# Moving six of eight single-token state steps of a Mamba-2 mixer from its own stage into six heads of the other mixer

## The chip, the cores and the metric

One Trainium2 chip, one core of it. The metric is the time of one execution on the device in microseconds. Of the kernel before there are three runs: median 1763.9 us, 1761.53 to 1765.04.

## What is computed

One decoder layer, fp32, for a prompt of 1024 tokens and for 8 sampled tokens (one new token each of 8 requests with states of their own): norm, one input projection into 6656 columns and 16 dt columns, two mixers side by side (HGRN2 with 8 heads, Mamba-2 with 16 heads of 64 in 2 groups), their gated norms, an output projection, a gated MLP with a causal convolution, a final norm. What matters here is the Mamba-2 step of the sampled tokens and the gate behind it. In the names of the kernel, for each pair of state-space heads j (0 to 7, four per group g):

```
state[b]  = state[b] * exp(dt*A)[b] + (dt*x)[b] outer B[g, b]      # 128 rows (2 heads x 64) by 128, b = 0..7
y[b]      = state[b] . C[g, b] + D * x[b]
gated     = y * silu(z)                                            # prompt columns likewise
mix       = gated * rsqrt(mean over the group's 512 rows of gated^2 + eps) * norm_w
```

The new states are an output (ssm_sample), and mix goes into the output projection with the HGRN2 heads' rows.

## The kernel before

Activations lie with channels on partitions and tokens along the free dimension: 1024 prompt columns and behind them 8 columns of the sampled tokens, 1032 in all, in three chunks of 344. Each weight tile comes as fp32, is split into a rounded part and a rest (L190 on ACT, L192 on DVE), and a product is three matmuls (L93). So an input job, 128 output columns, is 72 matmuls of 344 columns.

TensorE (PE) has an order written out by hand: a list of jobs, with streams of other work driven between their matmuls at a fixed number of pieces per matmul. The jobs are x8 and x10, x0 to x3, x9, x11, x4 to x7 (columns of x, B and C, with a convolution and a Silu at each job's end), z0 to z3, then f, q, v, sg of HGRN2 head 0, z4 to z7, then f to sg of heads 1 to 7, then the output projection (o8, o12, o0, o4), up, down and the last norm. `ssd(0)`, the chunked state-space scan of group 0, is driven beside x9 to x7; `ssd(1)` beside z0 to v0. `head(h)` is driven beside the input jobs of head h+1; head 7 beside the first output jobs. DVE, ACT and POOL get their order from the scheduler. Loads by `fetch` stand on the SP queue behind the last weight load.

In a chunk of the scan (`ssd_front`, `ssd_back`): xp is a transposed x tile, xdt its product with dt (L557), bt B and C products, csb the decay matrix (loaded, L541 and L546 on ACT, L560 on DVE), yo the part of the carried state, ecs its scaling (L577, L593), st the new state part, S the carried state (L583), yd the part within the chunk.

`ssm_decode(g, i)` (L628 to L647) is the step of the sampled tokens for j = 4g + i. In two halves of four tokens each it loads a state Sd and broadcast rows Bb and Cb (256 KB each), scales Sd on ACT (L641, four instructions), multiplies Bb (L642) and adds it to Sd (L643) on DVE, writes Sd, multiplies Cb on POOL (L645) and reduces it on DVE (L646); L647 adds D*x. It is called at the begin of x5, x7, z0 and z1 for group 0, and at that of z4 to z7 for group 1. `ssm_gate(g)` multiplies with silu(z) in the z jobs (L675, L676), all 1032 columns, and norms them.

A head with its decode rows goes: sample states of HGRN2 (Sh, L864 to L868), gates by halving (tt, L885 to L891), attention blocks a and am (L910 to L949), decode outputs od and odr (L956), kt and kv (L963 to L977) into the states SS, odp (L984), o from am, vt, q and SS, and the norm (hr_d, L999 to L1023). Tiles of the tag "e" (two, 1060 wide) carry wide rows in the x stage and in the first head; those of the tag "d" (four) carry a head's sample rows.

Of the kernel before, what the change touches and what calls it, by code (L numbers as in the profile page):

```python
# [39 lines left out]
QW = NT // 4  # L40
# [10 lines left out]
def hybrid_layer(  # L51
# [9 lines left out]
    V, A, G, PE, SP = nc.vector, nc.scalar, nc.gpsimd, nc.tensor, nc.sync  # L61
# [5 lines left out]
    dram = ctx.enter_context(tc.tile_pool(name="dscr", bufs=1, space=DRAM))  # L67
# [21 lines left out]
    def bank(s, tag="mx"):  # L89
        return psmx.tile([P, 512], F32, tag=tag, bufs=NBANK[tag], name=nm(s))  # L90

    def mm(out, lhsT, rhs, start=True, stop=True):
        PE.matmul(out, lhsT, rhs, start=start, stop=stop)  # L93
# [55 lines left out]
    def col(name, i=0):  # L149
        c = vlay[name] + i  # L150
        return vcol[:, c:c + 1]
# [20 lines left out]
    def fetch(dst, src):  # L172

        with tc.issue_after(last_w[0].ins):
            SP.dma_start(dst, src)
# [179 lines left out]
    def xbc_evict(j, ext, c, cs, ps):  # L355
        e = min(cs.stop, T)
        A.copy(ext[:, 3 + cs.start:3 + e], ps[:, :e - cs.start])
        if c == 2:
            V.tensor_copy(ext[:, 3 + T:3 + T + 32].rearrange("p (b r) -> p b r", r=4)[:, :, 3:4],
                          ps[:, T - cs.start:].unsqueeze(2))  # L360
            V.tensor_copy(last11[:, j, :], ps[:, CH - 11:])

    def xbc_close(j, ext):
        G.tensor_copy(ext[:, 3 + T:3 + T + 32].rearrange("p (b r) -> p b r", r=4)[:, :, 0:3],
                      bufT[:, j, :].rearrange("p (b r) -> p b r", r=3))
        n = T + 32
        acc = tl("big", "xbc")
        conv_tail(acc, ext, 4, "cw", "cb", j, XT, n)
        A.activation(acc[:, :T], acc[:, :T], AF.Silu)
        A.activation(acc[:, T:NT], acc[:, T + 3:T + 32:4], AF.Silu)  # L370
        return acc

    def xbc_job(j, put):
        ext = []
        def begin():
            ext.append(xbc_open())
            if j in (5, 7):
                ssm_decode(0, (5, 7).index(j))

        in_job(f"x{j}", OFF_X + j * P, lambda c, cs, ps: xbc_evict(j, ext[0], c, cs, ps), begin=begin, end=lambda: put(xbc_close(j, ext[0])))  # L380

# [20 lines left out]
    ones = keep.tile([P, P], F32, name="ones")  # L402
# [24 lines left out]
    for c, cs in enumerate(chunks):  # L427
        ps = psmm.tile([P, 512], F32, tag="mm", name=nm("dt"))
# [7 lines left out]
    dps = bank("dps", "nx")  # L436
# [177 lines left out]
    def d4(t):  # L614
        return t.rearrange("p (b n) -> p b n", n=P)
# [12 lines left out]
    def ssm_decode(g, i):  # L628
        j = g * 4 + i
        xdd = small.tile([P, 2, ND], F32, tag="xdd", name=nm("xdd"))  # L630
        xdec = Xg[g][i][:, T:NT]
        V.tensor_tensor(xdd[:, 0, :], xdec, ddb[:, 0, j, :], op=ALU.mult)
        for b0 in (0, 4):
            bs = slice(b0, b0 + 4)
            Bb, Cb = tl("d", "Bb")[:, :512], tl("d", "Cb")[:, :512]
            for t_, r in ((Bb, 2 * g), (Cb, 2 * g + 1)):
                fetch(t_, bc_d[r, bs].rearrange("b n -> (b n)").unsqueeze(0).to_broadcast([P, 512]))
            Sd = tl("ld", "Sd")
            fetch(d4(Sd), state_ssm[0, bs, 2 * j:2 * j + 2].rearrange("b h p n -> (h p) b n"))
            for b in range(4):  # L640
                A.activation(d4(Sd)[:, b, :], d4(Sd)[:, b, :], AF.Copy, scale=ddb[:, 1, j, b0 + b:b0 + b + 1])  # L641
            V.tensor_tensor(d4(Bb), d4(Bb), cb(xdd[:, 0, bs]), op=ALU.mult)  # L642
            V.tensor_tensor(Sd, Sd, Bb, op=ALU.add)  # L643
            SP.dma_start(ssm_sample[0, bs, 2 * j:2 * j + 2].rearrange("b h p n -> (h p) b n"), d4(Sd))
            G.tensor_tensor(Cb, Sd, Cb, op=ALU.mult)  # L645
            V.tensor_reduce(xdd[:, 1, bs], d4(Cb), axis=mybir.AxisListType.X, op=ALU.add)  # L646
        V.scalar_tensor_tensor(xdec, xdec, d_bc[:, j:j + 1], xdd[:, 1, :], op0=ALU.mult, op1=ALU.add)  # L647

    def rstd_of(dst, tmp, ps, n):

        A.activation(dst, ps, AF.Abs_reciprocal_sqrt, bias=epsc, scale=1.0 / n)
        V.scalar_tensor_tensor(tmp, ps, n * EPS, dst, op0=ALU.add, op1=ALU.mult)
        V.scalar_tensor_tensor(tmp, tmp, -0.5 / n, dst, op0=ALU.mult, op1=ALU.mult)
        V.scalar_tensor_tensor(dst, tmp, 1.5, dst, op0=ALU.add, op1=ALU.mult)

    gr_d = dram.tile([2, 4, QW], F32, name="gr_d")

    def ssm_gate(g):
        acc = []

        def z_job(i):
            j = g * 4 + i

            def begin():
                if i == 0:
                    acc.append(tl("g", "gacc"))
                if g:
                    ssm_decode(1, i)
                elif i < 2:
                    ssm_decode(0, i + 2)  # L670

            def evict(c, cs, ps):
                Y = Xg[g][i][:, cs]
                sz = tl("z", "sz")[:, :CH]
                A.activation(sz, ps, AF.Silu)  # L675
                V.tensor_tensor(Y, Y, sz, op=ALU.mult)  # L676
                if i == 0:
                    A.activation(acc[0][:, cs], Y, AF.Square)
                else:
                    A.activation(sz, Y, AF.Square)  # L680
                    (V if g or i == 3 else G).tensor_tensor(acc[0][:, cs], acc[0][:, cs], sz, op=ALU.add)
                if i == 3 and c == NCH - 1:
                    after(36, rstd)
            in_job(f"z{j}", OFF_Z + j * P, evict, begin=begin)

        def rstd():
            ps = bank("ms", "nx")
            for q in range(4):
                mm(ps[32 * q:32 * q + 32, :QW], ones[:, 0:32], acc[0][:, q * QW:(q + 1) * QW])
            nt = tl("z", "nt")  # L690
            rstd_of(nt[:, :QW], tl("z", "nt")[:, :QW], ps[:, :QW], 512)
            SP.dma_start(gr_d[g], nt[::32, :QW])
            after(36, rows)

        def rows():
            fetch(acc[0][:, :NT], gr_d[g].rearrange("a t -> (a t)").unsqueeze(0).to_broadcast([P, NT]))
            after(20, lambda: spread(tail(), 6))

        def tail():
            for i in range(4):  # L700
                j = g * 4 + i
                Y = Xg[g][i][:, :NT]
                V.scalar_tensor_tensor(Y, Y, col("sn", j), acc[0][:, :NT], op0=ALU.mult, op1=ALU.mult)
                SP.dma_start(mix_d[8 + j], Y)
                yield

        for i in range(4):
            z_job(i)
# [132 lines left out]

    def head(h, t):
        f, k, q, v, sg = (t[n] for n in ("f", "k", "q", "v", "sg"))


        dps = bank("vd", "nx")
        PE.transpose(dps[:ND, :P], v[:, T:NT], ident)
# [11 lines left out]
        for b0 in (0, 4):  # L859
            bs = slice(b0, b0 + 4)  # L860
            ds = slice(T + b0, T + b0 + 4)
            Sd, vb = tl("ld", "Sh"), tl("d", "vb")[:, :512]
            fetch(d4(Sd), state_hgrn[0, bs, h].rearrange("b k v -> k b v"))
            fetch(vb, vd_d[h, bs].rearrange("b n -> (b n)").unsqueeze(0).to_broadcast([P, 512]))  # L864
            G.tensor_tensor(d4(vb), d4(vb), cb(k[:, ds]), op=ALU.mult)
            V.tensor_tensor(d4(Sd), d4(Sd), cb(f[:, ds]), op=ALU.mult)
            G.tensor_tensor(Sd, Sd, vb, op=ALU.add)
            SP.dma_start(hgrn_sample[0, bs, h].rearrange("b k v -> k b v"), d4(Sd))  # L868
            Sds.append(d4(Sd))

# [75 lines left out]
        scale(6, pair[1], pair[1])  # L946
        for b in (0, 64):
            A.copy(am[b:b + 32, :, b + 32:b + 64], c32(ps[:, :256])[b:b + 32])
        A.copy(am[0:64, :, 64:P], p6[0:64, :].rearrange("p (c t) -> p c t", t=64))  # L949
# [6 lines left out]
        V.tensor_copy(odr, ops[:, :P])  # L956
        yield 3.5

        for hf in range(2):
# [24 lines left out]
        V.tensor_copy(od[:, 0, :], dps[:, :ND])  # L984
        A.activation(od[:, 1, :], dps[:, :ND], AF.Square)
        yield 3.2


        for hf in range(2):
# [529 lines left out]
```

## Time and profile before

| | |
|---|---|
| median of 3 runs | 1763.9 us |
| the profiled execution | 1764.9 us, of it 1763.2 us of span |
| PE busy | 1709.8 us (97%) |
| DVE, ACT, POOL busy | 1097.8, 778.7, 478.8 us |
| mean granted clock of TensorE | 0.995 |
| waits of PE between 160 and 240 us | 8.0 us in five |
| waits of PE between 440 and 800 us | 0.8 us in one |
| longest wait of PE between 800 and 1000 us | 4.5 us |

A row of the waits reads: engine, line, what it waited for, total us, times, longest us. A row of a timeline reads: start in us, duration in us, engine, line, operation, out<-in, shape, count, and in brackets the idle time of the engine ahead of it with what ended it. A row of the windows has the stretch, its length, then busy us and instructions (x) of PE, PEld (weight loads), DVE, ACT and POOL, then the granted clock of TensorE, the share of the DMA engines and GB/s. SPq is the queue of SP that issues DMAs.

### The profile page before, as it was taken

What the parts mean: (1) busy time and instruction counts of PE and PEld (TensorE: products, weight loads), DVE (VectorE), ACT (ScalarE), POOL (GpSimd) and SP (SyncE); (2) the same over time, 40 slices, a digit from 0 to 9 for tenths busy, and PEclk for the clock granted to TensorE, in tenths of its full rate; (3) what the DMA queues carried; (4) which work ended last, traced back from release to release, by engine and by line L of the source; (5) the groups of instructions that cost most, each with busy time, mean ns of one, the idle gap of its engine ahead of it and who ended that gap; (6) DMA issues with size and microseconds to landing.
All of it is one profiled execution on the core that took longest, in us unless ns stands there. A gap on an engine that the chain in (4) does not pass through costs nothing. (4 is left out here: it accounts for less than half of the span.)

```text
span 1763.2 us, 38543 instructions
## 1 busy us (share of the span) xinstructions
PE 1709.8 (97%) x16115; PEld 1659.4 (94%) x16115; DVE 1097.8 (62%) x1978; ACT 778.7 (44%) x1422; POOL 478.8 (27%) x485
## 2 busy tenths in 40 slices
PE   7999899999999999999799999999999999999998
PEld 6998789899999999999799989999999999999997
DVE  6668966566554554566636687776667767445545
ACT  7577686444434344344423374343333434111114
POOL 2103231111110110111220355666666664000002
PEclk9999999999999999999999999999999999999999
DMA  5355644553232332234336832222222226422312
GB/s 166 65 148 149 173 120 143 167 169 120 83 93 57 98 87 72 77 110 144 114 115 210 250 123 73 73 85 82 88 73 73 79 82 214 153 83 78 98 61 97
DMA packets 250132, 200.23 MB, mean 114 GB/s; under 512 B 47252, under 2 KB 220870, under 8 KB 249942
## 3 DMA queue, kind: packets, MB, share of 16 engines
q1 hardware_dynamic: 249670, 197.68, 37.0%
q8 instruction: 126, 2.06, 0.5%
q14 instruction: 48, 0.39, 0.1%
q0 software_dynamic: 288, 0.10, 0.0%
HBM read 155.17 MB, written 46.95 MB: 115 GB/s over the span
## 5 line engine op out<-in xcount | busy, mean ns | idle before, releaser
L93 PE MATMUL mm<-hl,wh 128*128 128x344 f32 x1248 | 406.1, 326 | 0.0
L93 PE MATMUL mm<-hh,wh 128*128 128x344 f32 x1248 | 405.6, 326 | 0.0
L93 PE MATMUL mm<-hh,wl 128*128 128x344 f32 x1248 | 402.8, 323 | 0.8 <-issue 0.8
L93 PEld LDWEIGHTS mm<-hl,wh 128*128 128x128 f32 x1248 | 236.1, 189 | 4.8 <-issue 4.2
L93 PEld LDWEIGHTS mm<-hh,wh 128*128 128x128 f32 x1248 | 236.1, 189 | 4.2 <-issue 3.4
L93 PEld LDWEIGHTS mm<-hh,wl 128*128 128x128 f32 x1248 | 236.3, 189 | 1.4 <-issue 1.2
L190 ACT CAST wh<-ws 128x1024 fp32r<-128x1024 f32 x96 | 100.6, 1048 | 254.9 <-PE dn L93 134.9
L93 PE MATMUL ub<-uh,wh 128*128 128x258 f32 x704 | 199.5, 283 | 4.2 <-DVE fext L1332 2.7
L93 PE MATMUL ub<-uh,wl 128*128 128x258 f32 x704 | 198.7, 282 | 0.0
L93 PE MATMUL ub<-ul,wh 128*128 128x258 f32 x704 | 198.6, 282 | 0.0
L93 PE MATMUL dn<-ah,wh 128*128 128x256 f32 (+1 forms) x640 | 181.1, 283 | 2.0 <-DVE x L1449 2.0
L93 PE MATMUL dn<-al,wh 128*128 128x256 f32 (+1 forms) x640 | 180.6, 282 | 0.0
L93 PE MATMUL dn<-ah,wl 128*128 128x256 f32 (+1 forms) x640 | 180.1, 281 | 0.0
L192 DVE TENSOR_TENSOR wl<-ws,wh 128x1024 fp32r<-128x1024 f32 x88 | 108.8, 1236 | 78.5 <-ACT wh L190 77.7
L93 PE MATMUL ua<-uh,wh 128*128 128x258 f32 x528 | 149.3, 283 | 1.5 <-DVE val L1344 1.3
L93 PE MATMUL mm<-mh,wh 128*128 128x258 f32 x512 | 146.9, 287 | 3.0 <-ACT x L1077 1.8
L93 PE MATMUL ua<-ul,wh 128*128 128x258 f32 x528 | 149.1, 282 | 0.0
L93 PE MATMUL ua<-uh,wl 128*128 128x258 f32 x528 | 148.4, 281 | 0.0
L93 PE MATMUL mm<-ml,wh 128*128 128x258 f32 x512 | 145.4, 284 | 0.9 <-DVE ml L1037 0.9
L93 PE MATMUL mm<-mh,wl 128*128 128x258 f32 x512 | 145.2, 284 | 0.0
L93 PEld LDWEIGHTS ub<-uh,wh 128*128 128x128 f32 x704 | 133.0, 189 | 4.9 <-DVE fext L1332 2.9
L1282 DVE TENSOR_TENSOR wl<-wt,wh 128x512 fp32r<-128x512 f32 x88 | 89.1, 1031 | 73.8 <-ACT wh L1281 73.8
(353 smaller groups left out, 3981.9 us busy)
## 6 DMA issues: line engine op xcount, KB each, us to landing
ws<-in_w_in_dram SPq DMA_DIRECT2D x52, 512.0 KB
ws<-in_w_up_dram SPq DMA_DIRECT2D x44, 512.0 KB
ws<-in_w_out_dram SPq DMA_DIRECT2D x24, 512.0 KB
act_d<-val SPq DMA_DIRECT2D x22, 516.0 KB
al<-act_d SPq DMA_DIRECT2D x22, 516.0 KB
ws<-in_w_down_dram SPq DMA_DIRECT2D x22, 512.0 KB
ml<-mix_d SPq DMA_DIRECT2D x48, 172.0 KB
csb<-cs_d SPq DMA_DIRECT2D x32, 256.0 KB
```

The source lines that it names most:

```text
L93: PE.matmul(out, lhsT, rhs, start=start, stop=stop)
L190: A.copy(wh[:, :n], ws[:, :n])
L192: V.tensor_tensor(wl[:, :n], ws[:, :n], wh[:, :n].bitcast(F32), op=ALU.subtract)
L1282: V.tensor_tensor(lo[:, cs], sums[name], hi[:, cs].bitcast(F32), op=ALU.subtract)
```

## The change

The sampled tokens' columns leave the wide tiles: the Silu of the convolution writes them into a small tile xdk, silu(z) of those columns goes into szd by a POOL copy in the last chunk of each z job, and the wide gate covers 1024 columns. Two decodes (j = 0 and 1) remain `ssm_decode`, at the begin of z4 and z6. The other six run as `decode_beside` in heads 1 to 6: in one width of 1024 (Sd and Bb in the two "e" tiles, Cb in two "d" tiles); the loads behind the head's last write of HGRN2 sample states, the multiplies and the add behind odr and am, the reduces behind the od copy. After the fourth of a group (heads 2 and 6) `decode_gate` gates its columns, and 80 pieces later `decode_norm` norms them (matmul dgs) and writes them into mix_d. The diff, cut to its core:

```diff
+    xdk = const.tile([P, 8, ND], F32, name="xdk")
+    szd = const.tile([P, 8, ND], F32, name="szd")
...
-        A.activation(acc[:, T:NT], acc[:, T + 3:T + 32:4], AF.Silu)
+        A.activation(xdk[:, j, :] if j < 8 else acc[:, T:NT], acc[:, T + 3:T + 32:4], AF.Silu)
...
-            if j in (5, 7):
-                ssm_decode(0, (5, 7).index(j))
...
+    def decode_beside(g, i):
+
+        j = g * 4 + i
+        xdd = small.tile([P, 2, ND], F32, tag="xdd", name=nm("xdd"))
+        xdec = xdk[:, j, :]
+        Sd, Bb = tl("e", "Sd")[:, :T], tl("e", "Bb")[:, :T]
+        Cb = [tl("d", "Cb")[:, :512] for _ in range(2)]
...
+        def load(behind):
+            with tc.issue_after(behind.ins):
+                SP.dma_start(d8(Sd), state_ssm[0, :, 2 * j:2 * j + 2].rearrange("b h p n -> (h p) b n"))
+                SP.dma_start(Bb, bc_d[2 * g].rearrange("b n -> (b n)").unsqueeze(0).to_broadcast([P, T]))
+                for q in range(2):
+                    SP.dma_start(Cb[q], bc_d[2 * g + 1, 4 * q:4 * q + 4].rearrange("b n -> (b n)").unsqueeze(0).to_broadcast([P, 512]))
...
+        def front(behind, behind_a):
+            V.tensor_tensor(xdd[:, 0, :], xdec, ddb[:, 0, j, :], op=ALU.mult)
+            with tc.issue_after(behind.ins):
+                V.tensor_tensor(d8(Bb), d8(Bb), xdd[:, 0, :].unsqueeze(2).to_broadcast([P, ND, P]), op=ALU.mult)
+            for b in range(ND):
+                with tc.issue_after(behind_a.ins):
+                    A.activation(d8(Sd)[:, b, :], d8(Sd)[:, b, :], AF.Copy, scale=ddb[:, 1, j, b:b + 1])
+            V.tensor_tensor(Sd, Sd, Bb, op=ALU.add)
+            SP.dma_start(ssm_sample[0, :, 2 * j:2 * j + 2].rearrange("b h p n -> (h p) b n"), d8(Sd))
+            for q in range(2):
+                G.tensor_tensor(Cb[q], Sd[:, q * 512:(q + 1) * 512], Cb[q], op=ALU.mult)
...
+        def back(behind):
+            for q in range(2):
+                with tc.issue_after(behind.ins):
+                    V.tensor_reduce(xdd[:, 1, 4 * q:4 * q + 4], d4(Cb[q]), axis=mybir.AxisListType.X, op=ALU.add)
+            V.scalar_tensor_tensor(xdec, xdec, d_bc[:, j:j + 1], xdd[:, 1, :], op0=ALU.mult, op1=ALU.add)
+            if i == 3:
+                decode_gate(g)
...
+    def decode_gate(g):
+        js = slice(4 * g, 4 * g + 4)
+        dg = small.tile([P, 6, ND], F32, tag="dg", bufs=1, name=nm("dg"))
+        V.tensor_tensor(xdk[:, js, :], xdk[:, js, :], szd[:, js, :], op=ALU.mult)
+        V.tensor_tensor(dg[:, 0:4, :], xdk[:, js, :], xdk[:, js, :], op=ALU.mult)
+        V.tensor_reduce(dg[:, 4, :], dg[:, 0:4, :].rearrange("p j b -> p b j"), axis=mybir.AxisListType.X, op=ALU.add)
+        after(80, lambda: decode_norm(g, js, dg))
+
+    def decode_norm(g, js, dg):
+        ps = bank("dgs", "nx")
+        mm(ps[:, :ND], ones, dg[:, 4, :])
+        rstd_of(dg[:, 4, :], dg[:, 5, :], ps[:, :ND], 512)
+        for j in range(js.start, js.stop):
+            V.scalar_tensor_tensor(xdk[:, j, :], xdk[:, j, :], col("sn", j), dg[:, 4, :], op0=ALU.mult, op1=ALU.mult)
+        SP.dma_start(mix_d[8 + js.start:8 + js.stop, :, T:NT].rearrange("j p b -> p j b"), xdk[:, js, :])
...
-                if g:
-                    ssm_decode(1, i)
-                elif i < 2:
-                    ssm_decode(0, i + 2)
+                if g and i % 2 == 0:
+                    ssm_decode(0, i // 2)
...
+                if c == NCH - 1:
+                    G.tensor_copy(szd[:, j, :], sz[:, n:])
...
+        step_ = decode_beside((h + 1) // 4, (h + 1) % 4) if 1 <= h <= 6 else None
...
+            step_[0](kept_)
...
+            step_[1](held, turned_)
...
+            step_[2](held)
```

PE's order differs only in two added matmuls dgs and in widths of the gate's norm. What moves on the others, first on DVE beside the scan of group 0 (jobs x6 and x7): xbc are x tiles, S and ecs as above. Before:

```order
L596 SCALAR_TENSOR_TENSOR xbc_1184<-xbc_1184,d_bc,ecs_1921 128x128
L643 TENSOR_TENSOR Sd_2098<-Sd_2098,Bb_2094 128x512
L643 TENSOR_TENSOR Sd_2113<-Sd_2113,Bb_2109 128x512
L646 TENSOR_REDUCE xdd_2092<-Cb_2095 128x4
L646 TENSOR_REDUCE xdd_2092<-Cb_2110 128x4
L647 SCALAR_TENSOR_TENSOR xbc_992<-xbc_992,d_bc,xdd_2092 128x8
L632 TENSOR_TENSOR xdd_2478<-xbc_1184,ddb 128x8
L583 TENSOR_TENSOR S_2042<-S_2042,st_2040 128x512
L577 TENSOR_TENSOR ecs_2031<-yo_2034,ecs_2031 128x512
L552 TENSOR_TENSOR bt_1991<-bg_1988,tri 128x128
```

and now, the same chunk:

```order
L597 SCALAR_TENSOR_TENSOR xbc_1186<-xbc_1186,d_bc,ecs_1890 128x128
L553 TENSOR_TENSOR bt_1960<-bg_1957,tri 128x128
L561 TENSOR_TENSOR csb_1943<-csb_1943,bt_1960 128x512
L561 TENSOR_TENSOR csb_1949<-csb_1949,bt_1960 128x512
L584 TENSOR_TENSOR S_2011<-S_2011,st_2009 128x512
L578 TENSOR_TENSOR ecs_2000<-yo_2003,ecs_2000 128x512
L594 TENSOR_TENSOR ecs_2000<-yd_2014,ecs_2000 128x512
```

Adds, reduces and the small steps of the decode are gone between the xbc steps and S, and bt and csb now stand ahead of S.

Second, ACT in head 2, from the last am copy to the norm of the head. Before:

```order
L949 COPY am<-a_749_6122 64x8x64
L831 ACTIVATE v_6170<-mm_6171 128x344
L964 COPY kt_6205<-ktp_6206 128x512
L964 COPY kt_6212<-ktp_6213 128x512
L831 ACTIVATE v_6170<-mm_6197 128x344
L985 ACTIVATE od_6270<-odp_6268 128x8
L190 CAST wh_6298<-ws_6297 128x1024
```

and now:

```order
L1010 COPY am<-a_717_5969 64x8x64
L674 ACTIVATE Sd_5490<-Sd_5490,ddb 128x128 x8
L890 ACTIVATE v_6031<-mm_6032 128x344
L1027 COPY kt_6066<-ktp_6067 128x512
L1027 COPY kt_6073<-ktp_6074 128x512
L890 ACTIVATE v_6031<-mm_6058 128x344
L1048 ACTIVATE od_6131<-odp_6129 128x8
L190 CAST wh_6159<-ws_6158 128x1024
```

The eight scales of the state stand between am and the eviction of v, ahead of both kt copies.

Third, DVE in head 2 in the SS steps behind kv. Before:

```order
L977 SCALAR_TENSOR_TENSOR SS_6247<-SS_6247,tt_5688,kv_6248 128x128 x2
L984 COPY od_6270<-odp_6268 128x8
L977 SCALAR_TENSOR_TENSOR SS_6247<-SS_6247,tt_5688,kv_6248 128x128
L1013 SCALAR_TENSOR_TENSOR sg_5520<-od_6270,vcol,sg_5520 128x8
L977 SCALAR_TENSOR_TENSOR SS_6257<-SS_6247,tt_5688,kv_6258 128x128
L977 SCALAR_TENSOR_TENSOR SS_6257<-SS_6257,tt_5688,kv_6258 128x128 x3
```

and now:

```order
L1040 SCALAR_TENSOR_TENSOR SS_6108<-SS_6108,tt_5535,kv_6109 128x128 x2
L1047 COPY od_6131<-odp_6129 128x8
L1040 SCALAR_TENSOR_TENSOR SS_6108<-SS_6108,tt_5535,kv_6109 128x128
L683 TENSOR_REDUCE xdd_5489<-Cb_5492 128x4
L1040 SCALAR_TENSOR_TENSOR SS_6118<-SS_6108,tt_5535,kv_6119 128x128
L683 TENSOR_REDUCE xdd_5489<-Cb_5493 128x4
L1040 SCALAR_TENSOR_TENSOR SS_6118<-SS_6118,tt_5535,kv_6119 128x128
L684 SCALAR_TENSOR_TENSOR xdk<-xdk,d_bc,xdd_5489 128x8
L1040 SCALAR_TENSOR_TENSOR SS_6118<-SS_6118,tt_5535,kv_6119 128x128
L693 TENSOR_TENSOR xdk<-xdk,szd 128x32
L1078 SCALAR_TENSOR_TENSOR sg_5355<-od_6131,vcol,sg_5355 128x8
L1040 SCALAR_TENSOR_TENSOR SS_6118<-SS_6118,tt_5535,kv_6119 128x128
```

The two reduces, the step of D and the first step of the gate now stand among the SS steps. (The wide multiply and the wide add stand further ahead, on both sides of the step qb that follows odr.)

More of the change, by code (lines that the diff above doesn't have):

```diff
@@ L630, in ssm_decode @@
         xdd = small.tile([P, 2, ND], F32, tag="xdd", name=nm("xdd"))
-        xdec = Xg[g][i][:, T:NT]
+        xdec = xdk[:, j, :]
         V.tensor_tensor(xdd[:, 0, :], xdec, ddb[:, 0, j, :], op=ALU.mult)
@@ L647, in ssm_decode, with d8 @@
         V.scalar_tensor_tensor(xdec, xdec, d_bc[:, j:j + 1], xdd[:, 1, :], op0=ALU.mult, op1=ALU.add)
+    def decode_beside(g, i):
+        j = g * 4 + i
+        xdd = small.tile([P, 2, ND], F32, tag="xdd", name=nm("xdd"))
+        xdec = xdk[:, j, :]
+        Sd, Bb = tl("e", "Sd")[:, :T], tl("e", "Bb")[:, :T]
+        Cb = [tl("d", "Cb")[:, :512] for _ in range(2)]
+        def d8(t):
+            return t.rearrange("p (b n) -> p b n", n=P)
+        def load(behind):
[22 more added lines that the diff above has]
+                decode_gate(g)
+        return load, front, back
@@ L654, in rstd_of @@
         V.scalar_tensor_tensor(dst, tmp, 1.5, dst, op0=ALU.add, op1=ALU.mult)
-    gr_d = dram.tile([2, 4, QW], F32, name="gr_d")
+    gr_d = dram.tile([2, 4, 256], F32, name="gr_d")
     def ssm_gate(g):
@@ L666, in begin @@
                     acc.append(tl("g", "gacc"))
-                if g:
-                    ssm_decode(1, i)
-                elif i < 2:
-                    ssm_decode(0, i + 2)
+                if g and i % 2 == 0:
+                    ssm_decode(0, i // 2)
             def evict(c, cs, ps):
+                cs = slice(cs.start, min(cs.stop, T))
+                n = cs.stop - cs.start
                 Y = Xg[g][i][:, cs]
@@ L675, in evict @@
                 A.activation(sz, ps, AF.Silu)
+                if c == NCH - 1:
+                    G.tensor_copy(szd[:, j, :], sz[:, n:])
+                sz = sz[:, :n]
                 V.tensor_tensor(Y, Y, sz, op=ALU.mult)
@@ L688, in rstd @@
             for q in range(4):
-                mm(ps[32 * q:32 * q + 32, :QW], ones[:, 0:32], acc[0][:, q * QW:(q + 1) * QW])
+                mm(ps[32 * q:32 * q + 32, :256], ones[:, 0:32], acc[0][:, q * 256:(q + 1) * 256])
             nt = tl("z", "nt")
-            rstd_of(nt[:, :QW], tl("z", "nt")[:, :QW], ps[:, :QW], 512)
-            SP.dma_start(gr_d[g], nt[::32, :QW])
+            rstd_of(nt[:, :256], tl("z", "nt")[:, :256], ps[:, :256], 512)
+            SP.dma_start(gr_d[g], nt[::32, :256])
             after(36, rows)
         def rows():
-            fetch(acc[0][:, :NT], gr_d[g].rearrange("a t -> (a t)").unsqueeze(0).to_broadcast([P, NT]))
+            fetch(acc[0][:, :T], gr_d[g].rearrange("a t -> (a t)").unsqueeze(0).to_broadcast([P, T]))
             after(20, lambda: spread(tail(), 6))
@@ L701, in tail @@
                 j = g * 4 + i
-                Y = Xg[g][i][:, :NT]
-                V.scalar_tensor_tensor(Y, Y, col("sn", j), acc[0][:, :NT], op0=ALU.mult, op1=ALU.mult)
-                SP.dma_start(mix_d[8 + j], Y)
+                Y = Xg[g][i][:, :T]
+                V.scalar_tensor_tensor(Y, Y, col("sn", j), acc[0][:, :T], op0=ALU.mult, op1=ALU.mult)
+                SP.dma_start(mix_d[8 + j][:, :T], Y)
                 yield
@@ L867, in head @@
             G.tensor_tensor(Sd, Sd, vb, op=ALU.add)
-            SP.dma_start(hgrn_sample[0, bs, h].rearrange("b k v -> k b v"), d4(Sd))
+            kept_ = SP.dma_start(hgrn_sample[0, bs, h].rearrange("b k v -> k b v"), d4(Sd))
             Sds.append(d4(Sd))
+        if step_:
+            step_[0](kept_)
         hb = [slice(0, 512), slice(512, T)]
@@ L948, in head @@
             A.copy(am[b:b + 32, :, b + 32:b + 64], c32(ps[:, :256])[b:b + 32])
-        A.copy(am[0:64, :, 64:P], p6[0:64, :].rearrange("p (c t) -> p c t", t=64))
+        turned_ = A.copy(am[0:64, :, 64:P], p6[0:64, :].rearrange("p (c t) -> p c t", t=64))
         ops = bank("od", "nx")
@@ L955, in head @@
         odr = small.tile([P, P], F32, tag="odr", bufs=1, name=nm("odr"))
-        V.tensor_copy(odr, ops[:, :P])
+        held = V.tensor_copy(odr, ops[:, :P])
+        if step_:
+            step_[1](held, turned_)
         yield 3.5
@@ L983, in head @@
         od = small.tile([P, 3, ND], F32, tag="dsq", name=nm("od"))
-        V.tensor_copy(od[:, 0, :], dps[:, :ND])
+        held = V.tensor_copy(od[:, 0, :], dps[:, :ND])
         A.activation(od[:, 1, :], dps[:, :ND], AF.Square)
         yield 3.2
+        if step_:
+            step_[2](held)
         for hf in range(2):
```

## Prediction

> **What bounds the kernel now.** I read the page first, then the waits of PE in stretches of the program, then the windows for the clock, then the timelines of DVE and ACT around each wait.
>
> ```profile
> span 1763.2 us, 38543 instructions
> PE 1709.8 (97%) x16115; PEld 1659.4 (94%) x16115; DVE 1097.8 (62%) x1978; ACT 778.7 (44%) x1422; POOL 478.8 (27%) x485
> ```
>
> PE is busy for all but 53.4 of 1763.2 us, and the change leaves its matmuls nearly as they are. So the only time to be won is where PE waits, and where its clock is cut. The waits of PE from 160 to 240 us (the state-space chunks beside x9 to z0), then the longest of 800 to 1000 us (it is in head 7):
>
> ```profile
> PE yo L93 <- DVE S L583: 2.0, 1, 2.0
> PE xp L555 <- ACT xbc L369: 2.0, 1, 2.0
> PE yd L93 <- DVE xdt L557: 1.5, 1, 1.5
> PE bg L548 <- DVE S L583: 1.3, 1, 1.3
> PE xp L555 <- DVE ecs L577: 1.2, 1, 1.2
> ...
> PE xtd L810 <- DVE odr L956: 4.5, 1, 4.5
> ```
>
> The five waits before 240 us sum to 8.0 us. What the waits do to the clock stands in the windows (the column behind POOL is the granted clock):
>
> ```profile
> 172.00:176.00 4.00, 2.85 (x27) 2.68 (x28) 3.96 (x5) 2.01 (x5) 2.49 (x2) 1.00 0.52 107
> 205.00:209.00 4.00, 2.43 (x10) 1.35 (x10) 4.00 (x7) 1.15 (x3) 1.88 (x2) 0.81 0.12 18
> 209.00:213.00 4.00, 4.00 (x29) 3.42 (x29) 3.79 (x8) 0.11 (x1) 1.77 (x2) 0.76 0.40 114
> 226.00:229.00 3.00, 1.36 (x6) 1.36 (x7) 0.93 (x2) 2.97 (x5) 0.00 (x0) 0.83 0.87 175
> 229.00:232.00 3.00, 3.00 (x13) 3.00 (x13) 0.18 (x1) 2.96 (x5) 1.04 (x1) 0.60 0.55 164
> 440.00:800.00 360.00, 359.16 (x4837) 345.06 (x4836) 183.72 (x350) 154.44 (x254) 31.43 (x24) 1.00 0.29 85
> ```
>
> Around the wait of 1.5 us (yd, at 173) the clock stays at 1.00. After each wait of 2.0 us it is cut: 4 × 0.19 + 4 × 0.24 = 1.7 us are lost at 205 to 213, and 3 × 0.17 + 3 × 0.40 = 1.7 us at 226 to 232. The five waits cost 8.0 + 3.4 = **11.4 us** together. In heads 1 to 6, the last row, PE is without work for 0.8 of 360 us, DVE works 184, ACT 154, POOL 31, and DMA has a share of 0.29.
>
> [...]
>
> **What each wait hangs on.** DVE, then ACT, at those places:
>
> ```profile
> 171.80 0.69 DVE L642 TENSOR_TENSOR Bb<-Bb,xdd 128x512 f32<-128x512 f32 x1 [2.83 <-DMA Bb<-bc_d]
> 172.41 0.68 DVE L557 TENSOR_TENSOR xdt<-xp,dt 128x512 f32<-128x512 f32 x1
> ...
> 185.56 1.28 DVE L643 TENSOR_TENSOR Sd<-Sd,Bb 128x512 f32<-128x512 f32 x2
> 188.03 0.69 DVE L646 TENSOR_REDUCE xdd<-Cb 128x4 f32<-128x512 f32 x1 [1.19 <-POOL Cb L645]
> 190.28 0.69 DVE L646 TENSOR_REDUCE xdd<-Cb 128x4 f32<-128x512 f32 x1 [1.56 <-POOL Cb L645]
> ...
> 191.34 0.68 DVE L583 TENSOR_TENSOR S<-S,st 128x512 f32<-128x512 f32 x1
> ...
> 193.34 1.28 DVE L560 TENSOR_TENSOR csb<-csb,bt 128x512 f32<-128x512 f32 x2
> ...
> 198.68 2.10 DVE L347 SCALAR_TENSOR_TENSOR xbc<-ext,vcol,xbc 128x1056 f32<-128x1056 f32 x1
> ...
> 203.32 1.30 DVE L347 SCALAR_TENSOR_TENSOR xbc<-ext,vcol,xbc 128x1056 f32<-128x1056 f32 x1
> ...
> 205.75 0.67 DVE L583 TENSOR_TENSOR S<-S,st 128x512 f32<-128x512 f32 x1
> ```
> ```profile
> 218.14 0.99 ACT L641 ACTIVATE Sd<-Sd,ddb 128x128 f32<-128x128 f32 x3 [0.94 <-DMA Sd<-in_state_ssm_dram]
> ...
> 220.55 0.39 ACT L641 ACTIVATE Sd<-Sd,ddb 128x128 f32<-128x128 f32 x1
> 221.61 1.28 ACT L541 ACTIVATE csb<-csb,cst 128x128 f32<-128x128 f32 x4 [0.68 <-DMA csb<-cs_d]
> ...
> 226.53 1.06 ACT L369 ACTIVATE xbc<-xbc 128x1024 f32<-128x1024 f32 x1
> ```
>
> - yd, 1.5 us: xdt stands behind a decode multiply that waited 2.83 us for its transfer. Without it xdt can start up to 2.8 us earlier, and the wait goes whole: 1.5.
> - xp behind ecs, 1.2 us: DVE again, 6 us on, with a conv step ahead of ecs that stays. I count 1.0 of it (0 to 1.2).
> - bg, 1.3 us: S at 191.34 stands behind the Sd adds (1.28), two reduces (1.38) and their waits for POOL (1.19 + 1.56), some 5.4 us of decode. In the new order bt and csb stand ahead of that S, 1.28 us and a small step, which leaves 3.8 us for a wait of 1.3. It goes whole: 1.3.
> - yo, 2.0 us: S at 205.75 stands behind the backlog of that, two more Bb multiplies (0.69 each), and conv steps stretched from 1.30 to 2.10. The conv steps stay. I count 1.7 of it (1.0 to 2.0); a rest of 0.3 costs no clock, so its 1.7 us of clock go too.
> - xp behind the Silu of x7, 2.0 us: four decode scales (0.99 + 0.39) and a wait of 0.94 go from ACT, 2.3 us, but the csb scales also wait for a transfer and may not come all of that earlier. I count 1.3 (0 to 2.0). The rest of 0.7 is below the waits that left the clock at 1.00, so 1.7 us of clock go.
>
> Sum: 1.5 + 1.0 + 1.3 + 1.7 + 1.3 = 6.8, with the clock 6.8 + 3.4 = **10.2 us** (if each counts at its low end, and one clock cut stays, 3.8 + 1.7 = 5.5; at the high end 11.4). Decodes also leave z5 and z7; no wait of PE hangs on them, so nothing. The two decodes left, beside z4 and z6, stand where two stood before. The small copies of eight gate columns on POOL, and the gate's passes over 1024 instead of 1032 columns, lie beside z jobs that show no wait for POOL: nothing.
>
> **What the heads have to take.** Each of heads 1 to 6 gets one decode. DVE, ACT, then PE and the DMA queue in head 2, which stands for the six:
>
> ```profile
> 549.36 0.69 DVE L866 TENSOR_TENSOR Sh<-Sh,f 128x512 f32<-128x512 f32 x1 [1.68 <-DMA Sh<-in_state_hgrn_dram]
> ...
> 557.53 0.17 DVE L984 COPY od<-odp 128x8 f32<-128x8 f32 x1
> ...
> 558.01 1.49 DVE L977 SCALAR_TENSOR_TENSOR SS<-SS,tt,kv 128x128 f32<-128x128 f32 x4
> ```
> ```profile
> 545.89 0.58 ACT L949 COPY am<-a 64x512 f32<-64x512 f32 x1
> 550.25 0.46 ACT L831 ACTIVATE v<-mm 128x344 f32<-128x344 f32 x1 [3.78 <-PE mm L93]
> 551.79 1.08 ACT L964 COPY kt<-ktp 128x512 f32<-128x512 f32 x2 [1.09 <-PE ktp L963]
> ```
> ```profile
> 555.42 1.95 PE L93 MATMUL kv<-vt,kt 128*128 128x128 f32 x16
> ...
> 562.47 0.39 PE L93 MATMUL o<-q,SS 128*128 128x128 f32 x2
> ```
> ```profile
> 525.10 3.22 SPq L868 DMA_DIRECT2D out_dram<-Sh  x2
> ...
> 546.08 1.86 SPq L175 DMA_DIRECT2D Sh<-in_state_hgrn_dram  x2
> ```
>
> ACT: eight scales of 0.39, 3.1 us, in a gap of 3.78 us behind am. They end at 549.6, before the eviction of v at 550.25 and kt behind it. DVE: the multiply and the add of twice the width (about 2 × 0.64 = 1.3 us each) fall beside gaps; the add ends near 550.9. POOL is idle and multiplies until 553.6. The reduces come behind the od copy at 557.5: two at 0.69 and a small step or three put 1.4 to 2.0 us among the SS steps, which end at 559.5 now and near 561.5 then. The first matmul that needs SS starts at 562.47, so the margin is 1 us and the work is **hidden: 0**. If that cover were gone, each us beyond it would stand in the way of PE.
>
> The loads are issued behind the Sh write, at 528.3, and wanted at 546.5: 18 us for 1.5 MB. Two Sh loads (0.5 MB) issued from 546.08 held DVE until 549.36 and 550.80, so 0.5 MB take at most 4.7 us and three times that 14.1 us. They land by 542.5. The w_in load behind them on SP's queue still has its time, since the DMA share is 0.29.
>
> The gate of four decodes adds, after heads 2 and 6, one matmul 128x8 (0.22 us a piece by the odp group, at most twice that with its weights), a table load and some eight DVE steps of 0.2 us.
>
> ```profile
> L93 PE MATMUL odp<-selod,odr x10: 175/216/256, 493.9 to 740.1; 128*128 128x8 f32 x10
> ```
>
> I count 0.4 us for the two matmuls. In head 3 the rest lies on engines that are idle half of the time, so nothing. In head 7 the small steps fall among the chain to odr (the 4.5 us wait), where DVE has hardly a gap:
>
> ```profile
> 834.00 2.56 DVE L1037 TENSOR_TENSOR ml<-ml,mh 128x344 fp32r<-128x344 f32 x3 [1.41 <-ACT mh L1036]
> ```
>
> They cost some 1.6 us ahead of a gap of 1.41 us, which takes them up, and one transpose of xs now stands ahead of that chain instead of in it. I take **0**, between −2 us (the transpose and a little of the wait saved) and +2 us (the steps added whole to the chain).
>
> Sum: 10.2 − 0.4 = **9.8 us** saved. The profiled execution took 1764.9 us (1763.2 of span and 1.7 around it), 1.0 above the median; so 1755.1 on its scale and **1754** on that of the median, 1763.9.
>
> **Rivals.**
> - *The waits stay in part.* Conv steps, evictions and csb multiplies still share DVE before 240 us, and POOL still stretches conv steps from 1.30 to 2.10. With each wait at its low end (5.5, less 0.4) it is 1759.
> - *The clock does not come back.* If it is cut there for something other than the two waits (PE has sparse stretches on either side of them), only the waits go: 1754 + 3.4 = 1757.5. Against it stands that it is 1.00 around yd's wait at 173, in the same kind of stretch. [...]
> - *Slower: a late state holds ACT in the heads.* The eight scales stand ahead of v and kt on ACT. If the state lands at 552.7 instead of 542.5, the scales end at 555.8, v and the kt copies (0.46 + 1.08) at 557.4, and kv, which starts at 555.42 now, waits 2.0 us. With the clock cut behind it that is 3.7 us a head, 22 us for six: **1776**. It decides from a landing at 550.7, 22 us after the issue; the Sh loads took 3 to 5 us, which speaks against it, and four loads in a row on one queue, with w_in behind them, speak for it.
> - *It is given back.* The change removes the waits, but head 7 gets longer (its DVE is full from 834 to 857, and the write of xdk stands between ml loads on SP's queue), by 5 us or more, or the freed DVE meets the next late transfer: 1762, no change.
>
> **Chances.** Forecast 0.54 (own range 1750.5 to 1757.5), partial 0.14, clock not back 0.05, given back 0.10, slower 0.17 (a third of it a milder case, one or two heads, near 1768). A measurement of this kernel can tell about 0.2%, 3.5 us, from no change. Faster by more than that takes the forecast, the clock case and nearly all of the partial case, 0.12 of it: 0.71. Same: the rest of that and the given back, 0.12. Slower: 0.17. The range goes from 1750 (all 11.4 and 2 in head 7 would be 1750.9) to 1765, which takes in the partial case and the one where all is given back and leaves out the slower ones.
>
> **What would show it.** Right: in 160 to 240 us the waits on L557 and S are gone, PE's clock is 0.97 or more, and head 2's PE waits for no engine. Wrong: a wait of o or kv on SS or kt in the heads, with DVE's reduces idle before them on Cb; a Sd scale waiting for its transfer ahead of v; xtd's wait in head 7 above 6.5 us; or the same waits before 240 us held by conv steps.

## The result, and the profile after

| | before | after |
|---|---|---|
| the runs known at the prediction, median | 1763.9 us (3 runs) | |
| all runs beside the result, median | 1766.75 us (8 runs) | 1754.27 us (8 runs) |
| ratio, with its 95% interval | | 0.9935, 0.9917 to 0.9953 |
| span of the profiled execution | 1763.2 us | 1752.2 us |

The forecast was 1754. From the profile page of the changed kernel:

```profile
span 1752.2 us, 38536 instructions
PE 1707.5 (97%) x16119; PEld 1659.1 (95%) x16119; DVE 1099.7 (63%) x1986; ACT 782.7 (45%) x1427; POOL 484.3 (28%) x493
```

PE's busy time fell by 2.3 us, the span by 11.0: the rest is idle time of PE that is gone. The same four things are now read again. First the windows over the scan of group 0 (PE busy first, the granted clock behind POOL):

```profile
160.00:200.00 40.00, 40.00 (x291) 36.83 (x286) 33.09 (x56) 26.72 (x54) 9.07 (x11) 1.00 0.47 115
200.00:240.00 40.00, 40.00 (x282) 37.25 (x280) 23.77 (x43) 32.66 (x62) 8.24 (x9) 1.00 0.33 90
```

PE is busy for all of the 80 us, where five waits stood, and the clock is 1.00 in both stretches. DVE shows why. These are xdt and the S of the two chunks that held yd and bg before:

```profile
176.01 0.68 DVE L594 TENSOR_TENSOR ecs<-yd,ecs 128x512 f32<-128x512 f32 x1
176.62 0.68 DVE L558 TENSOR_TENSOR xdt<-xp,dt 128x512 f32<-128x512 f32 x1
...
180.37 1.29 DVE L561 TENSOR_TENSOR csb<-csb,bt 128x512 f32<-128x512 f32 x2
182.10 0.69 DVE L584 TENSOR_TENSOR S<-S,st 128x512 f32<-128x512 f32 x1 [0.44 <-PE st L93]
```

S now waits 0.44 us for PE, where PE waited 1.3 us for S: the order of late and early has turned. Next, PE's waits up to 330 us:

```profile
PE sT L609 <- DVE S L584: 2.8, 1, 2.8
PE yo L93 <- DVE S L584: 1.1, 1, 1.1
PE yd L93 <- DVE xdt L558: 0.6, 1, 0.6
```

These stand at 302 to 318 us, at the end of the scan of group 1. The wait of sT was 2.5 us before and had the same cause, the Bb multiplies of the decode beside z4, which still stand ahead of S:

```profile
316.92 0.69 DVE L643 TENSOR_TENSOR Bb<-Bb,xdd 128x512 f32<-128x512 f32 x1 [0.92 <-DMA Bb<-bc_d]
317.53 0.68 DVE L584 TENSOR_TENSOR S<-S,st 128x512 f32<-128x512 f32 x1
```

The waits of yo and yd ahead of it were 0.3 us before and are 1.7 now. In the heads (440 to 800 us) the waits of PE are:

```profile
PE mm L93 <- issue: 1.5, 2, 0.9
PE a L93 <- issue: 1.1, 1, 1.1
```

PE waits for no engine there, as forecast, but "issue" (time in which PE waited for nothing that the profile shows) rose from 0.8 to 2.6 us. Last head 2, on ACT, DVE and PE:

```profile
535.27 2.46 ACT L674 ACTIVATE Sd<-Sd,ddb 128x128 f32<-128x128 f32 x8
539.19 0.46 ACT L890 ACTIVATE v<-mm 128x344 f32<-128x344 f32 x1 [1.46 <-PE mm L93]
```
```profile
547.65 0.68 DVE L683 TENSOR_REDUCE xdd<-Cb 128x4 f32<-128x512 f32 x1
548.25 0.34 DVE L1040 SCALAR_TENSOR_TENSOR SS<-SS,tt,kv 128x128 f32<-128x128 f32 x1
...
549.14 0.34 DVE L1040 SCALAR_TENSOR_TENSOR SS<-SS,tt,kv 128x128 f32<-128x128 f32 x1
```
```profile
551.40 0.39 PE L93 MATMUL o<-q,SS 128*128 128x128 f32 x2
```

The eight scales took 2.46 us (3.1 were counted) and ACT was idle for 1.46 us behind them. The last SS step ends at 549.5, 1.9 us before PE wants it (1 us was counted).

Where the 11.0 us came from, by the starts of the same matmuls in both profiles. One pair of them, before and after, as PE's timeline has them:

```profile
233.93 0.60 PE L555 MATMUL xp<-ident,xbc 128*128 128x128 f32 x4
```
```profile
220.69 0.60 PE L556 MATMUL xp<-ident,xbc 128*128 128x128 f32 x4
```

All of them:

| mark on PE | before | after | difference | since the mark above |
|---|---|---|---|---|
| yo of a chunk of ssd(0) | 158.41 | 157.63 | −0.8 | −0.8 |
| xp of the second chunk of ssd(1) | 233.93 | 220.69 | −13.2 | −12.5 |
| sT of group 1 | 329.83 | 318.27 | −11.6 | +1.7 |
| ktp of head 0 | 427.46 | 415.22 | −12.2 | −0.7 |
| ktp of head 6 | 795.22 | 785.08 | −10.1 | +2.1 |
| ktp of head 7 | 861.66 | 850.35 | −11.3 | −1.2 |
| the end | 1763.2 | 1752.2 | −11.0 | +0.3 |

So 12.5 us are won in the scan of group 0; 1.7 are lost at the end of the scan of group 1 and some 2 in heads 1 to 6. The experiments ask whether the places alone do it, which decode made which wait, what the heads cost and why, and whether the waits that are left can go.

### The profile page after: what moved, and what is told of

Its sections match the earlier page's. It is cut to its first block, busy times and chain, and to the rows that moved or that the text cites. A ratio compares the mean times of both kernels' runs of the same rounds, so it can differ in the third digit from the quotient of the medians.

```text
span 1752.2 us, 38536 instructions
## 1 busy us (share of the span) xinstructions
PE 1707.5 (97%) x16119; PEld 1659.1 (95%) x16119; DVE 1099.7 (63%) x1986; ACT 782.7 (45%) x1427; POOL 484.3 (28%) x493
## 3 DMA queue, kind: packets, MB, share of 16 engines
q8 instruction: 126, 2.06, 0.5%
```

## The experiments

Each time stands beside runs of the kernel before on the same chip (medians 1764.3 to 1765.3 us).

**after_again: the changed kernel once more.** No edit.

> The changed kernel once more, to put the next three beside it on one chip and to have a second profile of it. The theory says: 9 to 13 us below the kernel before (about 1754), no wait of PE between 160 and 240 us, the three waits of 0.6, 1.1 and 2.8 us between 300 and 320 us again. Open: the gaps named 'issue' of 1.1 us in head 2 (among the small matmuls a) and of 0.9 us in head 4. If they are of the kernel, they stand at the same places again; if they are chance or lost records, they stand elsewhere.

Measured: 1754.31 us, ratio 0.9939 (0.9923 to 0.9956). No wait in 160 to 240. The waits at 302 to 318 us are 0.2, 1.1 and 2.6. The gap in head 2 is there again, before the 50th of the 64 matmuls a; the profiles of the two executions:

```profile
525.41 0.28 PE L93 MATMUL a<-v,k 128*16 128x16 f32 x15 [1.12 <-issue]
```
```profile
524.70 0.28 PE L93 MATMUL a<-v,k 128*16 128x16 f32 x15 [1.14 <-issue]
```

That of head 4 is there too, smaller (0.3). They belong to the kernel. Head 7 doesn't repeat: from its first mark to the next (ktp of head 6 to that of head 7) it took 65.3 us in the first profile and 67.9 in the second, with a wait of xtd of 1.3 and 4.8 us. Differences of that size in head 7 mean nothing here.

**old_places: all of the change but the move.**

```diff
+            if j in (5, 7):
+                ssm_decode(0, (5, 7).index(j))
...
-                if g and i % 2 == 0:
-                    ssm_decode(0, i // 2)
+                if g:
+                    ssm_decode(1, i)
+                elif i < 2:
+                    ssm_decode(0, i + 2)
...
-            step_[0](kept_)
-            step_[1](held, turned_)
```

> All other edits of the change (tiles xdk and szd, the gate over 1024 columns, its own norm for the sampled columns), but the eight decodes at their old places: x5, x7, z0, z1 and z4 to z7, and none in the heads. Theory (the gain is the places alone): the waits on xdt, ecs, S and the Silu return, 6 to 9 us between 160 and 240 us, the clock there falls to about 0.91 in 200 to 240, and the time is within 3 us of the kernel before. Rival (the narrower gate and tiles bring part of the gain): 4 us or more below the kernel before.

Measured: 1765.41 us, ratio 0.9998 (0.9987 to 1.0009). The interval leaves the other edits some 2 us either way, so all but that of the gain is the move's. Its waits in 150 to 240 us:

```profile
PE yo L93 <- DVE S L586: 2.0, 1, 2.0
PE xp L558 <- ACT xbc L372: 1.9, 1, 1.9
PE sT L611 <- POOL Cb L648: 1.3, 1, 1.3
PE bg L551 <- DVE S L586: 1.3, 1, 1.3
PE xp L558 <- DVE ecs L580: 1.2, 1, 1.2
PE yd L93 <- DVE xdt L560: 0.4, 1, 0.4
```

They sum to 8.1 us, as in the kernel before, though not wait by wait: yd has 0.4 us instead of 1.5, and sT waits 1.3 us for a decode's multiply on POOL, which it did not before. The expectation was wrong on the clock, which was not cut behind the waits of 2.0 and 1.9 us:

```profile
200.00:240.00 40.00, 34.72 (x236) 32.03 (x235) 33.59 (x56) 29.50 (x60) 10.68 (x10) 1.00 0.58 158
```

**x5x7 and z0z1: two decodes put back.** In place of z4 and z6, the two `ssm_decode` begin with x5 and x7, or with z0 and z1; the heads stay as in the change.

```diff
-                if g and i % 2 == 0:
-                    ssm_decode(0, i // 2)
...
+            if j in (5, 7):
+                ssm_decode(0, (5, 7).index(j))
```

and z0z1, in place of the added lines:

```diff
+                if g == 0 and i < 2:
+                    ssm_decode(0, i)
```

> The changed kernel with the two decodes of z4 and z6 at x5 and x7. Theory (each wait belongs to one decode): the waits of yd on xdt, xp on ecs, bg and yo on S return, 4.5 to 6 us in 160 to 215, with a clock cut of 1.7 us or none behind the one of 2 us; xp does not wait for the Silu of x7; and the wait of sT goes (2.8 and 1.7 us). In sum 0 to 3.5 us above the changed kernel: 1754 to 1758. Rival (the waits come from four decodes together, backed up): less than 2 us of waits, and the time is 1751.

> The changed kernel with the two decodes of z4 and z6 at z0 and z1. Theory: of the five waits only that of xp for the Silu of x7 (2.0 us, with or without 1.7 us of clock) returns, and the wait of sT goes: 1 to 2.5 us below the changed kernel, 1752 to 1753. Rival (ACT has room once x7's decode is gone): no wait at all before 330 us, and the time is that of z5z7, 1750.

Measured: x5x7 1760.66 us, z0z1 1754.63 (one run each). The waits of x5x7, then of z0z1, in 150 to 240 us:

```profile
PE yo L93 <- DVE S L586: 1.3, 1, 1.3
PE bg L551 <- DVE S L586: 1.3, 1, 1.3
PE xp L558 <- DVE ecs L580: 1.2, 1, 1.2
PE yd L93 <- DVE xdt L560: 0.2, 1, 0.2
```
```profile
PE xp L556 <- ACT xbc L372: 1.8, 1, 1.8
PE yo L93 <- DVE S L584: 1.2, 1, 1.2
```

Each wait goes with its decode: x5 and x7 bring bg, xp on ecs and part of yo and yd, z0 and z1 bring the Silu and, not expected, a yo of 1.2 us. In both the wait of sT is gone. At the ktp of head 0 x5x7 is 3.4 us behind the changed kernel (418.65 against 415.22) and z0z1 2.5 us ahead of it (412.68), both as expected; behind that mark, where the two kernels do the same as the changed one, each loses another 3 us in its one run. So the x5x7 time is 2.7 us above what was expected at most. Its wait of sT is indeed gone, but waits of 1.5, 1.0, 0.8 and 1.1 us stand at 297 to 319 us in its profile, and what makes them was not tried.

**z5z7 and z5z7_b: the last two decodes behind the scan.**

```diff
-                if g and i % 2 == 0:
+                if g and i % 2:
```

> The two decodes that stayed in z jobs begin with z5 and z7 instead of z4 and z6, where the scan of group 1 has ended. Theory (DVE waits in front of S for the decode's transfer and PE for S): the wait of sT, 2.8 us, goes, and the clock cut behind it, 4 x 0.18 + 4 x 0.25 = 1.7 us; so 3.5 to 4.5 us below the changed kernel, 1750. Rival (the wait is that of S behind the chunk's own loads of ecs and csb, whatever else is there): the wait stays and the time is 1754, within 1 us of the changed kernel.

Measured: 1749.84 us, ratio 0.9922 (0.9907 to 0.9936), beside 0.9939 of the changed kernel on the same chip. The windows of its profile over both scans' ends:

```profile
160.00:240.00 80.00, 80.00 (x566) 74.19 (x563) 56.88 (x99) 59.65 (x116) 17.33 (x21) 1.00 0.40 102
300.00:340.00 40.00, 40.00 (x269) 37.88 (x269) 19.26 (x34) 16.98 (x34) 7.48 (x6) 1.00 0.37 107
```

The wait of sT and its clock cut (0.75 in 320 to 324 us of the changed kernel, 1.00 here) are gone, and the median is 4.5 us lower than the changed kernel's. The intervals overlap.

> z5z7 once more, beside early2 on one chip. 13 to 17 us below the kernel before; no wait of PE between 160 and 340 us; a gap of 0.4 to 1.2 us in head 2 at the 50th of 64 matmuls a.

Measured: 1750.7 us, ratio 0.9914 (0.9900 to 0.9929), whose interval lies below the ratio of the changed kernel in either set of runs (the intervals themselves overlap); in this profile a wait of yo of 0.5 us before 340 us, and in head 2 a gap of 1.40 us, above the range given.

**no_heads and loads_only: what the heads cost.** Both leave out part of the sampled tokens' steps for j = 2 to 7: no_heads all of it (loads, multiplies, adds, reduces, writes of the new states), loads_only all but the loads.

```diff
-            step_[1](held, turned_)
...
-            for q in range(2):
-                with tc.issue_after(behind.ins):
-                    V.tensor_reduce(xdd[:, 1, 4 * q:4 * q + 4], d4(Cb[q]), axis=mybir.AxisListType.X, op=ALU.add)
-            V.scalar_tensor_tensor(xdec, xdec, d_bc[:, j:j + 1], xdd[:, 1, :], op0=ALU.mult, op1=ALU.add)
```

and no_heads beside that:

```diff
-            step_[0](kept_)
```

> The changed kernel with the six decodes in the heads left out (their loads, multiplies, adds, writes and reduces; six of eight new states are not written), the gate's small steps kept. Theory (the heads hide them but for what the trace lost between head 1 and head 6, 2.3 us): 1 to 3 us below the changed kernel, with the start of kv and the kt transposes of heads 2 and 4 earlier by that. Rival A (they hide all): within 0.5 us. Rival B (they cost more than the marks show, by head 7's chain): 5 us or more below.

> The changed kernel with the loads of the six decodes in the heads kept and their work left out (no multiply, add, scale, write or reduce; six of eight new states are not written). Theory (what the heads cost is the loads, in front of PE's instructions): the gaps of 1.1 us in head 2 and of 0.3 to 0.9 us in head 4 are back at the same matmuls as in the changed kernel, and the heads 1 to 6 take as long as in it. Rival (the cost is the work on DVE and ACT): no gap there, as without the decodes.

Measured: 1753.42 and 1753.84 us, one run each, which can't tell them from 1754.3. The marks can. From the ktp of head 1 to that of head 2: 63.23 us before, 63.26 in old_places, 63.23 without the decodes, 63.90 with the loads alone, 64.47 and 64.48 in the changed kernel, 63.95 and 64.78 in z5z7. So the loads by themselves make a gap in head 2 (0.5 us, where the changed kernel has 1.1 and z5z7 0.6); the work on DVE, ACT and POOL isn't needed for it. In head 4 there was no gap with the loads alone, so for that one the expectation failed. (The gap at the 700s, in head 5, 0 to 2.0 us, is in the kernel before too, 0.8, and in no_heads 1.9: it doesn't need the change. With a gap of 2.0 us in z5z7_b and in early, head 5 took 64.2 and 64.5 us, where it took 61.5 before.)

**early, early2 and late: the loads elsewhere.** All three are z5z7 with the heads' loads moved; the first line pair of the diff is of early and early2, the next lines of early2, the last of late. early issues them behind the loads of vb; early2 also holds Cb back until odr (a one-column write by DVE, which the load must wait for); late holds Sd and Bb back until odr and leaves Cb early.

```diff
-            fetch(vb, vd_d[h, bs].rearrange("b n -> (b n)").unsqueeze(0).to_broadcast([P, 512]))
+            kept_ = fetch(vb, vd_d[h, bs].rearrange("b n -> (b n)").unsqueeze(0).to_broadcast([P, 512]))
...
+            for q in range(2):
+                with tc.issue_after(behind.ins):
+                    V.memset(Cb[q][:, 0:1], 0.0)
...
+            for t_ in (Sd, Bb):
+                with tc.issue_after(behind.ins):
+                    V.memset(t_[:, 0:1], 0.0)
```

> z5z7 with the loads of the six decodes in the heads issued behind the head's loads of vb, some 9 us earlier than behind the write of Sh. In the two profiles of the changed kernel and in z5z7, PE lost 0.6 to 1.1 us in head 2 before the 50th of 64 small matmuls a, while DMA engines had a share of 0.9; without the decodes it lost nothing there. Theory (PE's instructions come late behind the loads): the loads have ended by then, the gap in head 2 goes, head 2 (from kt's transposes of head 1 to those of head 2) takes 63.3 us instead of 63.95 to 64.5, and the time is 0.5 to 1.5 us below z5z7: 1748.5 to 1749.5. Rival (the gap is that of the matmuls a themselves or of work on DVE and ACT): the gap stays and the time is that of z5z7.

Measured: 1751.79 us, ratio 0.9924 (0.9912 to 0.9936). The gap stayed, 1.23 us. As worded the expectation failed: the Cb loads had remained behind the write of Sh, and from 518.4 to 519.6 us the queue of data transfers (q1) read 103 to 114% in each window of 0.2 us.

> As early, and the loads of Cb only behind the copy of odr, so that between the vb loads and the gap in head 2 no decode load is left. [...] Theory (the instruction load waits behind the decode's transfers): the third instruction load of head 2 comes some 3 us earlier against the head's start, the gap in head 2 goes, kt to kt from head 1 to head 2 is 63.2 to 63.4 us. Rival (the gap is set by something else in kernels with decodes in the heads): 0.4 to 1.2 us of gap again. In time at most 1 us below z5z7, which the chip can hardly tell; the marks decide.

Measured: 1751.49 us, ratio 0.9926 (0.9913 to 0.9939). The gap is gone: the 64 matmuls a run in one piece, and from ktp to ktp head 2 takes 63.20 us, head 4 60.61.

```profile
519.32 0.69 PE L93 MATMUL a<-v,k 128*16 128x16 f32 x64
```

In time it can't be told from z5z7_b beside it, as expected.

> z5z7 with the loads of the state and of Bb held back until odr is copied, some 20 us later than now (a small write of DVE holds them; Cb stays early). They then stand behind a weight load, and the scheduler puts the scales behind kt on ACT and the add ahead of SS on DVE. It is the slower rival of the prediction, made to happen: the state lands 7 to 9 us after odr, the scales end some 11 us after it, the add 12, POOL 15, and the SS steps, queued behind add and reduces on DVE, end 1 to 4 us after PE wants them. Theory: waits of o (or kv) for SS or DVE in each of heads 1 to 6, 1 to 4 us each and a clock cut behind some, 10 to 30 us above z5z7: 1760 to 1780. Rival (the heads have room for that too): below 1754.

Measured: 1749.77 us, one run. The theory fell. PE has no wait for SS, DVE or kt in any of heads 1 to 6. DVE in head 2 of late:

```profile
528.40 0.29 DVE L1018 COPY odr<-od 128x128 f32<-128x128 f32 x1
...
536.78 1.22 DVE L674 TENSOR_TENSOR Bb<-Bb,xdd 128x1024 f32<-128x1024 f32 x1 [1.25 <-DMA Bb<-bc_d]
538.10 1.23 DVE L678 TENSOR_TENSOR Sd<-Sd,Bb 128x1024 f32<-128x1024 f32 x1
...
540.73 0.69 DVE L686 TENSOR_REDUCE xdd<-Cb 128x4 f32<-128x512 f32 x1 [0.44 <-POOL Cb L681]
...
541.99 0.69 DVE L686 TENSOR_REDUCE xdd<-Cb 128x4 f32<-128x512 f32 x1 [0.32 <-POOL Cb L681]
...
543.91 0.34 DVE L1042 SCALAR_TENSOR_TENSOR SS<-SS,tt,kv 128x128 f32<-128x128 f32 x1
```

The add ended 10.6 us after odr, where 12 were expected, and the reduces waited 0.8 us for POOL. The SS steps ended at 544.2, behind the first o that takes SS at 543.62; but the o matmuls take SS slice after slice until 545.2, and PE didn't wait. I had counted all of SS as needed by the first of them.

> late once more, timed: it is the kernel with no wait in the scan, no gap in head 2 or head 4, and the decode's loads behind odr. Theory (the gaps of heads 2 and 4 were all that z5z7 lost by the decodes): 0.5 to 2 us below z5z7 (1749.8 and 1750.7 in its two jobs), 1748 to 1750, ratio to the kernel before 0.990 to 0.992; and the marks again at 63.2 us for head 2 and 60.6 for head 4. Rival (its one fast look was chance): a ratio of 0.9925 or above.

Measured: 1751.16 us, ratio 0.9921 (0.9903 to 0.9939), between the two expectations; marks again 63.24 and 60.54 us for heads 2 and 4. The gaps taken away are too small to show in the time. No version is clearly below z5z7.

## Why the prediction was right, and where it was not

The time (1754 against 1754.27) and the mechanism were right, in part by terms that cancel. By the marks, 13.2 us were won up to the end of the scan of group 0, where 10.2 were counted, and 1.2 in head 7, where nothing was; 1.7 were lost at the end of group 1, where nothing was counted, and 2.1 in the heads, where 0.4 was. That the time was hit to 0.3 us is luck: beside the result the kernel before came out at 1766.75 us instead of 1763.9, and by the ratio of 0.9935 the gain is 11.5 us, not 9.8.

- *The five waits go: 6.8 counted, 8.0 us found.* No rest stayed: the xp behind the Silu, of which 0.7 was to stay, and the yo, 0.3, went whole. On the former ACT had just enough: the Silu of x7 started at 214.43 and its x tile was wanted at 215.66. That the decodes made the waits is shown by old_places (8.1 us of waits return with the places alone), x5x7 and z0z1.
- *The clock: 3.4 counted; its size is not fixed.* In the profile of before it was cut behind both waits of 2.0 us, in old_places behind neither (1.00 from 200 to 240 us). Over seven profiles (before, old_places, the two of the changed kernel, no_heads, loads_only, z0z1) 11 waits of 1.8 to 2.8 us stand ahead of 340 us, and 7 were followed by a cut. The term was read from one execution as if it were the kernel's. The windows below are 3.41 us wide, as long as the cut in before, around the wait of yo (2.0 us) in before and then in old_places:

```profile
204.09:207.50 3.41, 1.41 (x12) 1.16 (x11) 3.41 (x6) 1.71 (x4) 1.00 (x1) 1.00 0.34 66
207.50:210.91 3.41, 3.41 (x18) 1.91 (x19) 3.41 (x7) 0.00 (x0) 1.35 (x2) 0.50 0.28 77
```
```profile
200.45:203.86 3.41, 2.75 (x18) 2.47 (x16) 3.41 (x5) 3.04 (x7) 0.00 (x0) 1.00 0.49 113
203.86:207.27 3.41, 2.07 (x12) 1.34 (x14) 3.41 (x7) 0.93 (x3) 1.51 (x2) 1.00 0.03 5
207.27:210.68 3.41, 2.71 (x26) 2.25 (x24) 3.41 (x7) 0.81 (x1) 1.46 (x2) 1.00 0.27 77
```

  In before PE is busy for 1.41 of the 3.41 us ahead of the cut, and the clock is 0.50 in the next 3.41. In old_places it is busy for 2.75, 2.07 and 2.71 us of the three windows, and the clock is 1.00 in all. So the same wait came with 1.7 us of lost clock in one execution and with none in the other; what decides between the two was not shown.
- *The marks show 12.5 us in the scan, against 8.0 + 3.4.* The 1.1 us left were not taken apart.
- *sT at z4 stays.* It did, 2.5 before and 2.8 and 2.6 after; z5z7 took it away. The waits of yo and yd ahead of it were put at nothing ("The two decodes left, beside z4 and z6, stand where two stood before") and grew from 0.3 us to 1.7 and 1.3. They stand in early and early2 too (1.7 and 1.4), where no decode begins with z4, so they aren't that decode's; what makes them was not tried.
- *The heads hide the decodes: 0 counted (and 0.4 for the two matmuls dgs), 2.1 us lost.* The margins on ACT and DVE were there and larger than counted, as late showed, whose add ends 70.3 us behind the ktp of head 1 instead of 63.4, at no cost. The step that failed is "the w_in load behind them on SP's queue still has its time, since the DMA share is 0.29": it looked for what else the loads could delay among data transfers only. The profile has one more queue ("q8 instruction", 126 packets, 2.06 MB, so 16 KB each), and in the changed kernel one of its loads falls into the stretch of the gap in head 2, a window of the DMA view from 521 to 524 us:

```profile
q1 hardware_dynamic: 825, 0.94, 93.7%
q8 instruction: 1, 0.02, 1.9%
```

  The other queue has the engines for 93.7% of these 3 us; loads_only shows that the decodes' loads are enough for a gap (head 2 took 63.90 us instead of 63.23), early2 that it goes when they are moved (63.20). That instructions come late behind them was the author's estimate; no run shows it.

- *Head 7 at 0: −1.2 in one profile, +1.5 in the other.* Within ±2, and not to be told from chance.

## What to carry to other kernels

Where one engine is busy for 97%, the time to be won is in the few places where it waits; find the instruction that holds what it waits for, and move that work to a stage where the same engines are idle half of the time, which cost 2 us for six decodes here against 12.5 won. Ask of the new place what the transfers, not only the instructions, will meet there. And take a clock cut from more than one execution before it becomes a term of a sum: here the same wait of 2.0 us cost 1.7 us of clock or none.

## What the runs showed of the hardware

The gap in head 2 is longer the later one load of the queue "q8 instruction" begins. Measured from the ktp of head 1, one load of 16 KB, the third behind 30 us, began in the window (0.2 us wide) whose start is given here, and PE's gap before the 50th of 64 small matmuls a (the 48th in x5x7) was:

| kernel | load at, us | gap, us |
|---|---|---|
| before, early2 | 43.6, 43.6 | none |
| late, late_b | 45.6, 45.4 | none |
| z0z1 | 46.6 | 0.38 |
| loads_only, z5z7 | 46.8, 46.8 | 0.53, 0.57 |
| x5x7 | 47.0 | 1.05 |
| after, after_again, early | 47.2, 47.2, 47.2 | 1.12, 1.14, 1.23 |
| z5z7_b | 47.6 | 1.40 |

In these profiles there is no gap up to 45.6, and from 46.6 to 47.6 it goes from 0.38 to 1.40 us. In early2 and late the decode's transfers were moved, the load stood at 43.6 and 45.6, and the gap was gone. Whether the later load makes the gap was not shown: no run moved that load alone, and the profile doesn't say whose instructions it brings.

The gaps in the other heads stand beside such a load too. From 300 to 1000 us the profiles of before and after have eight gaps of PE over 0.25 us that they put down to "issue", three and five, those of head 7 among them. Each ends 2.3 to 3.0 us behind the begin of one of these loads; of all matmuls in that stretch, 7% begin so far behind one. What makes these gaps was not tried.
